# The order of PSUM pools at the entry of attention, and two entries of the up projection, in a transformer block on one core

## The chip, the cores and the metric

The kernel runs on one core of a Trainium2 chip. The metric is the device time of one execution in microseconds (us), and lower is better. Engines are called as the profile calls them: PE is the matrix engine and PEld its weight load, DVE is VectorE, ACT is ScalarE, POOL is GpSimd, and SP is the queue that issues most loads. Each engine works off its own list of instructions in order; where an instruction waits, all behind it on the same engine wait too.

## The reference

One block for 1024 frames of 1024 features, in float32:

```python
h = rms_norm(x, norm1)
proj = h @ w_in                      # q, k, v of two attentions, forget gates, output gates
o_a = forgetting_attention(...)      # 8 heads x 64, causal, decay by sums of log f
o_b = chunk_band_attention(...)      # 8 heads x 64, own chunk of 64 and the 8 before it
merged = g_a * (o_a @ w_branch_a) + g_b * (o_b @ w_branch_b)
x = x + merged @ w_out
h2 = rms_norm(x, norm2)
x = x + square(relu(h2 @ w_up)) @ w_down      # w_up 1024 x 4096, w_down 4096 x 1024
return rms_norm(x, final_norm)
```

## The kernel before

Activations lie transposed, features on the 128 partitions and frames along the free axis in two halves `h` of 512. Every float32 operand is split into a high part (a rounding cast, names ending in `h` or starting with `wh`, `th`) and a low part (value minus high part, names ending in `l` or starting with `wl`, `tl`). A product is then three passes on PE: high x high, high x low, low x high (`product`, L216). The high part of a weight is cast on ACT, its low part is a subtraction on POOL (`split_w`, L163 and L165).

The large products are done in units by one level of Strassen's scheme. A unit (`strassen_steps`) takes four raw quarters of weights (`wr`, loaded from `wall`), makes four sums of them on POOL (`S1`, `S2`, `S3`, `S4`, at L186, L188, L203, L206), splits the seven operands, and runs seven products into four PSUM banks `u0` to `u3`. With activations called `B11, T2, T1, T3, B21, B22, T4`, the products come in the order A11, S2, S1, S3, A12, S4, A22, and DVE and ACT combine the banks between them (L577 to L590). When product 3 (S3) is done, bank 1 is final; products 4, 5 and 6 make banks 0, 2 and 3 final. Raw quarters have four buffers, sums three, and `wh` and `wl` six each, so the seventh weight of a unit, A22, takes the buffer of the first one, A11.

What sets the order of instructions: a scheduler arranges everything that isn't marked, by its own model of time. Instructions through `VO, TO, AO, GO, LO` keep the order in which the code is written. `tc.issue_after(x)` keeps an instruction behind `x`.

Two places matter here.

**The entry of attention.** The last unit of the projections (gate unit 7) works in the four banks of the PSUM pool `psd0`, while the first head's scores run between its products in other banks. Its result in bank `u3` is the last to be ready; DVE scales it (`zt`, L403), and ACT issues its store to `z_dram` (L406). When `psd0` is closed, three pools are opened over its four banks: `pst` (2 banks, transposed probabilities `pt`), `psv` (1 bank, the products `pv` of probabilities and values) and `psg` (1 bank, gate products, and each third `pt` in the first heads). A new tile in a bank waits for the last reader of the bank's old tile. Gate unit 7 has its result `u2` in the first bank, `u3` in the second, `u0` in the third and `u1` in the fourth, since the buffers of `psd0` are dealt out in turn and six single tiles came before the units. For each group of probabilities, PE transposes blocks into `pt` (each T of the order strings), ACT makes `th` (H), DVE makes `tl` (L), and PE multiplies with the values (P).

**The entry of the up projection.** The products with `w_out` are just over; DVE and ACT still make the operands of the first up unit from the last blocks. Unit 28 is the first of 16 units and unit 29 the second. Unit 28 starts on blocks 0 to 2 of its first four products (`START2`) and then takes block 3 of each, whose operands come last (`late_operands`, L1028 to L1037, splits at L278 and L279). After product 3 it does the column sums for the second norm (`norm2_stat`: PE multiplies the squares in `rstd` with `ones`, `n_s`, L266; DVE and ACT turn them into a reciprocal root, L239 to L243, L272, L273); after product 6 the root is spread over partitions (`n_b`) and copied to `rstd` (L1092), and only then do the results of unit 28 leave PSUM (L1101). The weights of unit 29 are held back by `behind=late`, where `lows` is the list of all instructions that made a low part `wl`. Right after unit 28, `lows[-1]` is `wl` of its A22, `lows[-3]` that of its A12.

Of the kernel before, what the change touches and what calls it, by code (L numbers as in the profile page):

```python
# [87 lines left out]
def hs(h):  # L88
    return slice(h * HALF, (h + 1) * HALF)
# [3 lines left out]
def hybrid_block(ctx: ExitStack, tc: tile.TileContext, xT, xN, g1, wall, wf, fb, relb, g2, g3, outT):  # L93
# [17 lines left out]
    def pool(stack, name, side, bufs=1, **kw):  # L111
        return stack.enter_context(tc.tile_pool(name=name, bufs=bufs, side=side, reuse_waits="tile", **kw))

    def psum(stack, name, bufs, side="left"):
        return stack.enter_context(tc.tile_pool(name=name, bufs=bufs, space=PSUM, side=side, reuse_waits="tile"))
# [43 lines left out]
    lows = []  # L159
# [13 lines left out]
    def strassen_w(u, eng, want=ALL):  # L173

        q, sums, out = {}, {}, {}

        def raw(n):
            if n not in q:
                q[n] = quarter(u, n)
            return q[n]  # L180

        def total(name):
            if name not in sums:
                t = sums[name] = wp.tile([P, HALF], F32, tag="ws", name=f"{name}_{u}", bufs=SUMS)
                if name == "S1":
                    eng.tensor_tensor(t, raw(3), raw(2), op=ALU.add)  # L186
                else:
                    eng.tensor_tensor(t, total("S1"), raw(0), op=ALU.subtract)  # L188
            return sums[name]

        if "S2" in want and "A12" in want:
            for n in (0, 1, 3, 2) if want[1] == "A12" else (0, 3, 2, 1):
                raw(n)
        for name in want:
            if name in ("A11", "A12", "A22"):
                src = raw(int(name == "A12") + 2 * int(name == "A22"))
            elif name in ("S1", "S2"):
                if "S2" in want:
                    total("S2")
                src = total(name)  # L200
            elif name == "S3":
                src = raw(3)
                eng.tensor_tensor(src, raw(0), src, op=ALU.subtract)  # L203
            else:
                src = total("S2")
                eng.tensor_tensor(src, raw(1), src, op=ALU.subtract)  # L206
            out[name] = split_w(src, f"{u}_{name}", eng=eng)
        return out

    def product(bank, first, pairs, part=False, eng=T):  # L210

        n = len(pairs) * 3
        t = 0
        for w, x in pairs:
            for wi, xi in ((0, 0), (0, 1), (1, 0)):
                done = eng.matmul(bank, w[wi], x[xi], start=(first and t == 0), stop=(t == n - 1 and not part),  # L216
                                  skip_group_check=part or not first)
                t += 1
        return done.ins
# [41 lines left out]
    def norm_stat(ps_pool, name, acc, eng=T):  # L261

        ps = ps_pool.tile([P, HALF], F32, tag="d", name=f"{name}_s")
        n = acc.shape[1] // P
        for c in range(n):
            eng.matmul(ps[:, c:c + 1], acc[:, c * P:(c + 1) * P], ones, start=True, stop=True)  # L266
        return rms(name, ps, n)

    def rms(name, ps, n=4):

        y, v, t = cpool.tile([P, 2, 4], F32, tag="nr", name=f"{name}_r", bufs=2)[:, 0, 0:n], ps[:, 8:8 + n], ps[:, 16:16 + n]
        V.tensor_scalar(v, ps[:, 0:n], EPS, None, op0=ALU.add)  # L272
        A.activation(y, ps[:, 0:n], AF.Sqrt, bias=epsb)  # L273
        newton(name, v, y, t)
        return y
# [10 lines left out]
    xstack, pstack, astack = ExitStack(), ExitStack(), ExitStack()  # L286
# [249 lines left out]
    def strassen_unit(*args, **kw):  # L536
        for _ in strassen_steps(*args, **kw):
            pass

    def strassen_steps(u, ps_pool, mk, out, start=(), between=None, before=None, cut=0, behind=(), eng=T):  # L540

        def weights(*args):
            with ExitStack() as order:
                for ins in behind:
                    order.enter_context(tc.issue_after(ins))
                return strassen_w(u, *args)

        ws = weights(V if between else G, ALL[:cut] if cut else FIRST if between else ALL)
        late, out_ = [], out
        if before:
            out = lambda *a: late.append(a)
        banks = {}
        for b in (0, 2, 3, 1) if between else range(4):
            banks[b] = ps_pool.tile([P, HALF], F32, tag="d", name=f"u{u}_{b}")
        p1, u2, c22 = mk("p1"), mk("u2"), mk("c22")
        done, steps = None, [(n, range(4)) for n in range(7)]
        if start:  # L560
            more = (0, 4, 1, 2, 3, 5, 6) if between else range(7)
            steps = [(n, range(3)) for n in start] + [(n, (3,) if n in start else range(4)) for n in more]
        for i, (n, ks) in enumerate(steps):
            if i >= cut:
                yield done
            if cut and i == cut:
                ws = weights(G, ALL[cut:])
            wn, xn, b, first = PRODS[n]
            wh, wl = ws[wn]
            done = product(banks[b], first and 0 in ks, [((wh[:, k, :], wl[:, k, :]), xop[xn, k]) for k in ks],  # L570
                           3 not in ks, eng if i >= cut else T)
            if 3 not in ks:
                continue
            if n == 3 and before:
                before[0]()
            if n == 0:
                A.copy(p1, banks[0])  # L577
            elif n == 1:
                V.tensor_tensor(u2, banks[1], p1, op=ALU.add)
            elif n == 2:  # L580
                V.tensor_tensor(c22, banks[2], u2, op=ALU.add)  # L581
            elif n == 3:
                V.tensor_tensor(banks[1], banks[3], c22, op=ALU.add)  # L583
                out(1, 1, banks[1])
            elif n == 4:
                if between:
                    between()
                out(0, 0, banks[0])
            else:
                V.tensor_tensor(banks[b], banks[b], u2, op=ALU.add)  # L590
                out(*((0, 1) if n == 5 else (1, 0)), banks[b])
        if before:
            before[1]()
            for a in late:
                out_(*a)
# [40 lines left out]
    def project_gate(g, **kw):  # L636
        return strassen_steps(U_GATE + g, psd[1 - next(units) % 2], etile,
                              lambda row, h, src: gate_out(src, 2 * g + row, h,
                                                          G if g in GPOOL and (row, h) != (0, 0) else V), **kw)
# [70 lines left out]
    o3 = [[opool.tile([P, HALF], F32R, tag=f"o3{t}{h}", name=f"o3{t}{h}") for t in "hl"] for h in range(2)]  # L710
    apq.append(pool(astack, "apq1", "right"))
    apv, ap0 = [pool(astack, n, "right") for n in ("apv", "ap0")]
    pst = psum(astack, "pst", 2)
    psv = psum(astack, "psv", 1)
    psg = psum(astack, "psg", 1)

    ab_w = {}

# [256 lines left out]
    psm = [psum(ctx, f"psm{n}", 4) for n in range(2)]  # L975
# [39 lines left out]
    accs = [rstd[:, hs(h)] for h in range(2)]  # L1015

    def etile3(name):
        p = ep2[len(ep2[1:]) * (next(turn) % 2)]
        return p.tile([P, HALF], F32, tag="e", name=name, bufs=8)
# [64 lines left out]
    ep2.append(pool(hstack, "ep3", "left"))  # L1084
    n2 = []

    def norm2_stat():
        n2.extend(norm_stat(psm[1], f"n2_{h}", accs[h]) for h in range(2))

    def norm2():  # L1090
        for h in range(2):
# [3 lines left out]
    late = ()  # L1095
    for u in range(16):
        got = {}

        def out(row, h, src):
            v = etile3("v")  # L1100
            V.scalar_tensor_tensor(v, src, 0.0, rstd[:, hs(h)], op0=ALU.max, op1=ALU.mult)  # L1101
            A.activation(v, v, AF.Square)  # L1102
            got[row, h] = v
            if (row, h) != (0, 1):
                store(a_dram[{(0, 0): XI["B11"], (1, 0): XI["B21"], (1, 1): XI["B22"]}[row, h], u], v)
            for n, a, b in {(0, 1): (("T1", (0, 1), (0, 0)), ("T3", (1, 1), (0, 1)), ("T2", (1, 1), "T1")),
                            (1, 0): (("T4", (1, 0), "T2"),)}.get((row, h), ()):
                t = got[n] = etile3("at")
                V.tensor_tensor(t, got[a], got[b], op=ALU.subtract)
                store(a_dram[XI[n], u], t)  # L1110

        strassen_unit(U_UP + u, psm[u % 2], etile3, out, start=() if u else START2, before=None if u else (norm2_stat, norm2),
                      behind=late)

        late = () if u else (lows[-3].ins,)
    hstack.close()
    kstack.close()

# [42 lines left out]
    accs, begun = [rstd[:, hs(h)] for h in range(2)], set()  # L1161
# [185 lines left out]
```

## Time and profile before

| what | time |
|---|---|
| median of three timed runs | 1427.55 us (1426.97 to 1428.85) |
| the profiled execution | 1430.48 us |
| its span, first to last instruction | 1428.5 us |
| granted clock of PE, mean | 0.995 of full speed |
| PE busy | 1400.7 us (98%) |
| DVE, POOL, ACT busy | 885.1, 812.2, 706.6 us |

Times inside the execution are counted from the start of its span. In rows of the timeline the first number is the start, the second the duration, then engine, line, operation, output<-inputs, shape and count; in brackets stands how long the engine was idle before it and what ended that. Matmuls follow each other at shorter distances than their durations, since they overlap in the array. A granted clock (PEclk) of 0.50 means that PE ran at half speed.

### The profile page before, as it was taken

To read this page: it belongs to the slowest core of one execution; us is meant where nothing else is said; L and a number is where in the kernel's file an instruction comes from. 1 tells how busy PE (TensorE), PEld (TensorE's weight loads), DVE (VectorE), ACT (ScalarE), POOL (GpSimd) and SP (SyncE) were. 2 spreads that over 40 slices of the span, in tenths; PEclk is the share of its full clock that TensorE was granted. 3 is DMA by queue.
4 is the path that set the end of the run, shared out by engine and by line. 5 is a ranking of instruction groups with operands and counts; after the bars stand their busy time and mean duration, and the time that the engine had idled before them with its cause. 6 is when DMAs were issued, how large, how long until landed. Compare 5 with 4: busy or idle time off the path is not lost.

```text
span 1428.5 us, 20411 instructions
## 1 busy us (share of the span) xinstructions
PE 1400.7 (98%) x6676; PEld 1168.7 (82%) x6676; DVE 885.1 (62%) x1389; ACT 706.6 (49%) x1361; POOL 812.2 (57%) x639
## 2 busy tenths in 40 slices
PE   9999999999999999999999999999999999999996
PEld 6788888888878888888888888888888888888885
DVE  7756445543258887776655855545555559998644
ACT  8534333343358887775454543333333444444653
POOL 0477777778832233113724677777777545567564
PEclk9999999999999999999999999999999999999998
DMA  8546667773454668886644244444444784678263
GB/s 282 154 116 194 187 196 219 204 198 121 147 169 147 185 209 248 246 257 215 213 162 146 68 166 151 155 154 157 148 154 169 252 269 156 178 234 225 81 221 118
DMA packets 132820, 259.75 MB, mean 182 GB/s; under 512 B 18594, under 2 KB 20642, under 8 KB 129642
## 3 DMA queue, kind: packets, MB, share of 16 engines
q1 hardware_dynamic: 84570, 172.79, 38.6%
q10 hardware_dynamic: 44944, 77.78, 17.2%
q0 software_dynamic: 3200, 7.88, 2.5%
q8 instruction: 52, 0.85, 0.2%
q14 instruction: 54, 0.44, 0.1%
HBM read 172.70 MB, written 85.69 MB: 181 GB/s over the span
## 4 chain that ended last, share of the span: by engine, by line
PE 87%; DVE 3%; issue 3%; ACT 2%; POOL 2%; DMA 2%; SPq 0%; POOLq 0%; ACTq 0%; DVEq 0%
PE u L216 44%; PE dS L216 12%; PE dA L216 5%; PE o L216 5%; PE s L106 5%; PE pv L106 4%; PE pt L106 3%; PE m L106 3%; PE m L216 3%; POOL wl_A L165 1%; PE u L106 1%; DMA xg<-xT 1%; DMA xT<-a_dram 1%; ACT p L106 1%; PE vtp L627 0%
## 5 line engine op out<-in xcount | busy, mean ns | idle before, releaser
L165 POOL TENSOR_TENSOR wl_A<-wr,wh_A 128x512 fp32r<-128x512 f32 x118 | 158.4, 1352 | 94.0 <-ACT wh_A L163 77.0
L165 POOL TENSOR_TENSOR wl_S<-S,wh_S 128x512 fp32r<-128x512 f32 x102 | 136.0, 1337 | 32.9 <-ACT wh_S L163 32.3
L163 ACT CAST wh_S<-S 128x512 fp32r<-128x512 f32 x105 | 64.6, 621 | 114.0 <-PE u L216 53.9
L163 ACT CAST wh_A<-wr 128x512 fp32r<-128x512 f32 x105 | 65.0, 620 | 88.7 <-PE u L216 55.8
L106 DVE TENSOR_TENSOR tl<-pt,th 128x512 fp32r<-128x512 f32 (+1 forms) x144 | 90.5, 641 | 25.9 <-ACT th L106 24.4
L165 POOL TENSOR_TENSOR wl_S<-ks,wh_S 128x512 fp32r<-128x512 f32 x48 | 69.1, 1501 | 53.4 <-ACT wh_S L106 50.0
L590 DVE TENSOR_TENSOR u<-u,u 128x512 f32<-128x512 f32 x70 | 48.8, 698 | 76.0 <-PE u L216 73.6
L106 ACT ACTIVATE p<-s,mn 128x640 f32<-128x640 f32 (+3 forms) x120 | 84.4, 703 | 16.6 <-DVE mn L106 15.5
L106 ACT CAST th<-pt 128x512 fp32r<-128x512 f32 (+1 forms) x144 | 77.6, 551 | 24.5 <-PE pt L106 22.3
L106 PE MATMUL pt<-ident,p 128*128 128x128 f32 x528 | 78.1, 274 | 1.2 <-DVE zt L403 1.1
L186 POOL TENSOR_TENSOR S<-wr,wr 128x512 f32<-128x512 f32 x35 | 46.3, 1324 | 54.8 <-DMA wr<-wall 50.2
L106 PEld LDWEIGHTS pt<-ident,p 128*128 128x128 f32 x528 | 62.2, 141 | 11.0 <-PE pv L106 2.0
L106 PE MATMUL s<-qk 128*128 128x384 f32 (+2 forms) x192 | 58.6, 360 | 8.1 <-ACT p L106 7.3
L165 POOL TENSOR_TENSOR wl_A<-ka,wh_A 128x512 fp32r<-128x512 f32 x32 | 45.1, 1419 | 35.6 <-ACT wh_A L106 34.1
L278 ACT CAST qkh<-qk 128x512 fp32r<-128x512 f32 x32 | 19.9, 621 | 87.5 <-DMA qk_dram<-qkl 34.2
L1102 ACT ACTIVATE v<-v 128x512 f32<-128x512 f32 x64 | 40.4, 632 | 45.1 <-DVE v L1101 42.9
L924 POOL TENSOR_TENSOR on<-on,lo 128x512 f32<-128x512 f32 x7 | 9.0, 1292 | 92.7 <-ACT lo L106 92.7
L106 PE MATMUL pv<-th,v 128*128 128x512 f32 (+3 forms) x180 | 61.3, 348 | 0.1
L583 DVE TENSOR_TENSOR u<-u,c 128x512 f32<-128x512 f32 x35 | 24.5, 699 | 59.4 <-PE u L216 57.3
L106 PE MATMUL pv<-tl,v 128*128 128x512 f32 (+3 forms) x180 | 56.8, 335 | 0.2 <-DVE tl L106 0.2
L1101 DVE SCALAR_TENSOR_TENSOR v<-u,rstd 128x512 f32<-128x512 f32 x64 | 43.9, 688 | 20.1 <-PE u L216 18.1
L581 DVE TENSOR_TENSOR c<-u,u 128x512 f32<-128x512 f32 x35 | 24.2, 691 | 50.7 <-PE u L216 48.9
(445 smaller groups left out, 4742.2 us busy)
## 6 DMA issues: line engine op xcount, KB each, us to landing
wr<-wall SPq DMA_DIRECT2D x233, 256.0 KB
a_dram<-at ACTq DMA_DIRECT2D x64, 256.0 KB
xT<-a_dram SPq DMA_DIRECT2D x64, 256.0 KB
qk<-qk_dram SPq DMA_DIRECT2D x15, 1024.0 KB
qk_dram<-qkh ACTq DMA_DIRECT2D x96, 128.0 KB
a_dram<-v ACTq DMA_DIRECT2D x48, 256.0 KB
xB<-a_dram SPq DMA_DIRECT2D x44, 256.0 KB
z_dram<-zt ACTq DMA_DIRECT2D x32, 256.0 KB
```

Of the source, the lines that this page charges most:

```text
L106: return lambda *a, **kw: tc.keep_in_program_order(getattr(self.eng, name)(*a, **kw))
L163: (act.tensor_copy if act is G or act is V else act.copy)(wh, src)
L165: lows.append(eng.tensor_tensor(wl, src, wh.bitcast(F32), op=ALU.subtract))
L186: eng.tensor_tensor(t, raw(3), raw(2), op=ALU.add)
L216: done = eng.matmul(bank, w[wi], x[xi], start=(first and t == 0), stop=(t == n - 1 and not part), skip_group_check=part or not first)
L278: A.copy(dst[0], src)
L581: V.tensor_tensor(c22, banks[2], u2, op=ALU.add)
L583: V.tensor_tensor(banks[1], banks[3], c22, op=ALU.add)
L590: V.tensor_tensor(banks[b], banks[b], u2, op=ALU.add)
L924: G.tensor_tensor(o, o, lows_o[pr], op=ALU.add)
L1101: V.scalar_tensor_tensor(v, src, 0.0, rstd[:, hs(h)], op0=ALU.max, op1=ALU.mult)
L1102: A.activation(v, v, AF.Square)
```

## The change

The three PSUM pools are opened in the order `psg`, `psv`, `pst`. The sums for the second norm are emitted half by half, the first behind product 3 and the second behind product 4 of unit 28. The weights of unit 29 are held behind the last low part of unit 28, not the third from last.

```diff
-            if n == 3 and before:
-                before[0]()
+            if n in (3, 4) and before:
+                before[0](n - 3)
...
-    pst = psum(astack, "pst", 2)
-    psv = psum(astack, "psv", 1)
-    psg = psum(astack, "psg", 1)
+    psg, psv, pst = [psum(astack, n, b) for n, b in (("psg", 1), ("psv", 1), ("pst", 2))]
...
-    def norm2_stat():
-        n2.extend(norm_stat(psm[1], f"n2_{h}", accs[h]) for h in range(2))
+    def norm2_stat(h):
+        n2.append(norm_stat(psm[1], f"n2_{h}", accs[h]))
...
-        late = () if u else (lows[-3].ins,)
+        late = () if u else (lows[-1].ins,)
```

The number of instructions is the same on every engine, and their order on PE, DVE and SP too. It differs in two places, on POOL and on ACT, both at the entry of the up projection; at the entry of attention one wait differs.

POOL at the entry of the up projection, before (`28` and `29` are the units, the last number of a name is a buffer's own):

```order
L165 TENSOR_TENSOR wl_28_S4_8664<-S2_28_8640,wh_28_S4_8662 128x512
L186 TENSOR_TENSOR S1_29_8845<-wr29_3_8834,wr29_2_8836 128x512
L188 TENSOR_TENSOR S2_29_8844<-S1_29_8845,wr29_0_8832 128x512
L203 TENSOR_TENSOR wr29_3_8834<-wr29_0_8832,wr29_3_8834 128x512
L165 TENSOR_TENSOR wl_28_A22_8668<-wr28_2_8632,wh_28_A22_8666 128x512
L165 TENSOR_TENSOR wl_29_A11_8842<-wr29_0_8832,wh_29_A11_8840 128x512
L165 TENSOR_TENSOR wl_29_S2_8850<-S2_29_8844,wh_29_S2_8848 128x512
```

And the same stretch now:

```order
L165 TENSOR_TENSOR wl_28_S4_8664<-S2_28_8640,wh_28_S4_8662 128x512
L165 TENSOR_TENSOR wl_28_A22_8668<-wr28_2_8632,wh_28_A22_8666 128x512
L186 TENSOR_TENSOR S1_29_8845<-wr29_3_8834,wr29_2_8836 128x512
L165 TENSOR_TENSOR wl_29_A11_8842<-wr29_0_8832,wh_29_A11_8840 128x512
L188 TENSOR_TENSOR S2_29_8844<-S1_29_8845,wr29_0_8832 128x512
L203 TENSOR_TENSOR wr29_3_8834<-wr29_0_8832,wr29_3_8834 128x512
L165 TENSOR_TENSOR wl_29_S2_8850<-S2_29_8844,wh_29_S2_8848 128x512
```

The low part of unit 28's A22 now stands ahead of all three sums of unit 29 (the row at L203 is S3), and that of unit 29's A11 behind the first sum. On ACT the two casts `wh_29_S2` and `wh_29_S1` moved behind the two small roots of the norm (L273); on PE the column sums of both halves stand where they stood.

PE at the entry of attention, before, with the engines that each row waits for (DMAHW2 is a transfer):

```order
L106 MATMUL pt<-ident,p_0_3953 128x128 [waits DVE_49]
L106 MATMUL pt<-ident,p_1_3959 128x128
L106 MATMUL pt<-ident,p_2_3981 128x128
L106 MATMUL pt<-ident,p_3_3987 128x128
L106 MATMUL pt<-ident,p_1_3959 128x128 [waits DVE_49]
L106 MATMUL pt<-ident,p_2_3981 128x128
L106 MATMUL pt<-ident,p_3_3987 128x128 x2
L106 MATMUL pt<-ident,p_2_3981 128x128
L106 MATMUL pt<-ident,p_3_3987 128x128
L106 MATMUL pv<-th,v_4109 128x512 [waits DMAHW2_49,Activation_49]
```

And the last of these rows now:

```order
L106 MATMUL pv<-th,v_4109 128x512 [waits DMAHW2_49,DVE_49,Activation_49]
```

The second group of transposes (its first row is the fifth) had the bank of `u3` before; now it has that of `u1`, and the bank of `u3` goes to `pv`, which therefore waits for DVE as well.

## Prediction

> **What bounds the kernel now.** First the busy times of the page, then the waits of PE over the whole execution, longest first; the rows give engine, tile and line that waited, what ended the wait, us in total, count, longest.
>
> ```profile
> PE 1400.7 (98%) x6676; PEld 1168.7 (82%) x6676; DVE 885.1 (62%) x1389; ACT 706.6 (49%) x1361; POOL 812.2 (57%) x639
> PE s L106 <- ACT p L106: 7.3, 11, 0.9
> ...
> PE pt L106 <- DVE zt L403: 1.1, 1, 1.1
> PE u L216 <- ACT p L577: 0.9, 1, 0.9
> PE u L216 <- DVE T2l L279: 0.8, 1, 0.8
> PE dA L106 <- POOL wl_A L165: 0.7, 1, 0.7
> ```
>
> PE bounds the kernel, and the change can only pay where PE waits or runs slowly. The change touches two of these rows: 1.1 us for a bank of `pt` and 0.8 us for `T2l`. Third I asked for the granted clock in stretches of 3.41 us (start:end, us, then busy us and count of PE, PEld, DVE, ACT, POOL, then PEclk):
>
> ```profile
> 416.93:420.35 3.42, 2.25 (x15) 1.56 (x13) 1.68 (x4) 1.82 (x4) 0.00 (x0) 1.00 0.85 278
> 423.76:427.17 3.41, 2.07 (x12) 1.22 (x10) 1.91 (x7) 2.41 (x7) 0.00 (x0) 1.00 0.35 102
> 427.17:430.58 3.41, 3.16 (x12) 2.97 (x13) 2.37 (x7) 2.52 (x7) 0.00 (x0) 0.50 0.41 154
> 806.05:809.46 3.41, 2.65 (x21) 2.43 (x20) 3.34 (x3) 2.45 (x3) 3.41 (x3) 1.00 0.07 27
> 809.46:812.87 3.41, 3.41 (x10) 2.63 (x9) 3.38 (x5) 0.26 (x1) 3.41 (x4) 0.50 0.36 127
> 812.87:816.28 3.41, 3.41 (x17) 2.78 (x16) 1.84 (x13) 0.95 (x3) 2.54 (x3) 1.00 0.02 5
> ```
>
> Twice PE runs at half speed for 3.41 us, each time right behind 3.41 us in which it did little. The second time is at the up projection's entry: 10 matmuls where 17 start in the next stretch.
>
> **The change, part one: the pools of attention.** The entry of attention in order of time:
>
> ```profile
> 417.71 0.60 PE L106 MATMUL pt<-ident,p 128*128 128x128 f32 x4
> 418.64 0.69 DVE L403 TENSOR_TENSOR zt<-u,rstd 128x512 f32<-128x512 f32 x1
> 419.37 0.33 ACTq L406 DMA_DIRECT2D z_dram<-zt  x1
> 419.39 0.87 PE L106 MATMUL pt<-ident,p 128*128 128x128 f32 x6 [1.08 <-DVE zt L403]
> 419.74 1.35 ACT L106 CAST th<-pt 128x512 fp32r<-128x512 f32 x3 [1.28 <-DVE zt L403]
> 420.38 0.49 PE L106 MATMUL pv<-th,v 128*128 128x512 f32 x1
> 421.10 0.51 PE L106 MATMUL pv<-tl,v 128*128 128x512 f32 x1 [0.23 <-DVE tl L106]
> ```
>
> PE loses 1.08 us because the second `pt` has the bank of `u3`, which DVE reads until 419.33. Now it gets the bank of `u1`, free long before, and the six transposes can follow the first four at 418.15. But the first four were done near 418.3 already, and ACT still cast them only at 419.74: ahead of the cast in ACT's list stands the store of `zt` (L406), which waits for the same `zt` and takes 0.33 us to issue. That order is unchanged. So the first `th` comes at 419.74 as before, the second and third directly behind it (three casts in 1.35 us leave no gap), and `pv` at 420.38. The wait that `pv` gets on DVE ended at 419.33, a microsecond earlier. The 1.08 us that vanish behind the transposes come back ahead of `pv`. Value taken: 0. Bounds: a gain of 1.08 us if ACT were not held by the store, which its own idle row (1.28 us, ended by `zt`) excludes; a loss through the clock, below. When attention is over, the pools of the next stage take the same banks with two waits placed otherwise; PE waits for none of them in the list above, so 0.
>
> **Part two: the sums for the norm, half by half.** On PE the column sums keep their places, on DVE too. Only two casts of unit 29 on ACT come behind the roots. 0.
>
> **Part three: the weights of unit 29.** Here POOL's list changes. What DVE pays for POOL, first at a quiet place, then at the entry:
>
> ```profile
> 787.03 0.68 DVE L279 TENSOR_TENSOR T1l<-xg,T1h 128x512 fp32r<-128x512 f32 x1
> 788.75 1.31 POOL L165 TENSOR_TENSOR wl_S<-S,wh_S 128x512 fp32r<-128x512 f32 x1 [2.19 <-ACT wh_S L163]
> 788.84 1.78 DVE L279 TENSOR_TENSOR B22l<-xg,B22h 128x512 fp32r<-128x512 f32 x1
> ...
> 797.74 1.75 POOL L165 TENSOR_TENSOR wl_S<-S,wh_S 128x512 fp32r<-128x512 f32 x1
> 801.25 1.74 POOL L186 TENSOR_TENSOR S<-wr,wr 128x512 f32<-128x512 f32 x1 [1.76 <-DMA wr<-wall]
> 806.36 3.41 POOL L165 TENSOR_TENSOR wl_A<-wr,wh_A 128x512 fp32r<-128x512 f32 x2
> 801.77 1.78 DVE L279 TENSOR_TENSOR B22l<-xg,B22h 128x512 fp32r<-128x512 f32 x1
> 805.17 1.77 DVE L279 TENSOR_TENSOR T2l<-t,T2h 128x512 fp32r<-128x512 f32 x1
> 801.88 0.62 ACT L278 CAST T2h<-t 128x512 fp32r<-128x512 f32 x1
> 804.33 0.62 ACT L163 CAST wh_A<-wr 128x512 fp32r<-128x512 f32 x1 [1.82 <-PE u L216]
> 805.96 0.28 PE L266 MATMUL n_s<-ones,rstd 128*128 128x1 f32 x2
> 807.00 0.50 PE L216 MATMUL u<-T2l,wh_S 128*128 128x512 f32 x1 [0.77 <-DVE T2l L279]
> 807.57 1.62 PE L266 MATMUL n_s<-ones,rstd 128*128 128x1 f32 x14
> 809.05 0.48 PE L216 MATMUL u<-B21h,wh_A 128*128 128x512 f32 x1
> ```
>
> The same low part on DVE takes 0.68 us while POOL idles (787.03) and 1.78 us while POOL subtracts (788.84). From 801.25 POOL makes the three sums of unit 29, and on DVE `B22l`, `T3l` and `T2l` take about 1.75 us each; `T2l` ends at 806.94, and PE waits 0.77 us for it.
>
> Now the sums stand behind `wl_28_A22`, whose cast runs on ACT at 804.33, because it needs the buffer that PE reads until then. So POOL idles from 799.5 to 804.95. DVE's three low parts run free: `B22l` from 801.77, then `T3l`, then `T2l` (its cast ends at 802.50), each 0.68 us: `T2l` ends at 801.77 + 3 x 0.68 = 803.8. PE wants it behind the first two records of `n_s`, at 805.96 + 2 x 0.11 = 806.18. The wait is gone with 2.4 us to spare, and PE gains 807.00 - 806.18 = 0.82 us. Bounds: 0 (contention at some other place ends at the same time) and 0.82; I take 0.8, as the margin is larger than one contended operation adds (1.1 us).
>
> What comes late instead: POOL starts the sums of unit 29 at 806.25, five microseconds later. The needs stand here:
>
> ```profile
> 809.73 3.14 POOL L165 TENSOR_TENSOR wl_S<-S,wh_S 128x512 fp32r<-128x512 f32 x2
> 814.19 1.28 POOL L165 TENSOR_TENSOR wl_S<-wr,wh_S 128x512 fp32r<-128x512 f32 x1
> 820.64 0.48 PE L216 MATMUL u<-B11h,wh_A 128*128 128x512 f32 x1
> 823.48 0.39 PE L216 MATMUL u<-T2h,wh_S 128*128 128x512 f32 x1
> ```
>
> From 804.95 it has `wl_28_A22`, S1, `wl_29_A11`, S2, S3, `wl_29_S2`: six operations of 1.3 to 1.75 us, so `wl_29_S2` is ready between 812.8 and 815.5 (before: between 811 and 812). PE takes it as the third pass of a product that began at 823.48 and may now begin 2.5 us earlier, at 821. Five microseconds are left. The casts `wh_29_S2` and `wh_29_S1`, behind the roots, need those sums anyway. SP's loads for units 29 and 30 wait for the same POOL operations: the load of `wr29_1` for `wl_28_A22`, now 1.8 us earlier; the first of unit 30 for `wl_29_A11`, about the same. Nothing is lost, 0.
>
> **The clock.** In 806.05 to 809.46 PE ran two 512-column matmuls and sixteen one-column ones, then two more of 512. At full rate these start 0.227 us apart (17 or 18 in 3.41 us), so the four are 0.9 us of work. After that PE ran at half speed for 3.41 us, which costs half of it, 1.70 us. Without the wait, `B21h` starts at 808.24, the same stretch holds 2 + 5 matmuls, 1.6 us. The other stretch that was followed by half speed (423.76) holds 1.17 us counted by columns, and 416.93, which was not, about 1.25 us. So 1.6 us should not trip it: up to 1.70 us more. But the two half-speed stretches begin 382.29 us apart, 112.0 times 3.413: the gate looks at a fixed grid of stretches, and where the grid falls differs between executions. The poor period, 805.96 to 809.05, must nearly fill a cell; sliding the cell, this holds for about 1.1 to 1.5 us of 3.41, an estimate of 4 executions in 10.
>
> [...]
>
> **The sum.** Against the profiled execution (1430.48 us, both half-speed stretches): 0.82 + 1.70 = 2.5 us, to 1428.0. The profile stands 2.93 us above the median 1427.55, nearly two stretches (3.4 us), and the three runs spread over 1.88 us, about one. So the median run probably had none at this place, and there only the 0.8 us count: 1426.75. With the lower level of the two nearer runs (1426.97, 1427.55; mean 1427.26) it is 1426.45. I take 1426.5. From 820 on PE waits almost nowhere (the 0.7 us for `wl_A` in the list is the one wait between units and the tail), so the gain reaches the end.
>
> **Rivals.**
> 1. *The stretch goes in the median too* (0.8 + 1.7): 1425.0. For it: the profiled execution. Against it: the distance of the median from the profile.
> 2. *The clock is not moved by the wait*, because the sixteen one-column sums, which stay, are enough to trip it; the median loses 0.8 us alone, 1426.75. For it: the sums took 1.62 us of the poor cell; against it: 1.6 us of matmuls would now stand beside them. It differs from the forecast by less than the runs spread, and I count it with it. [...]
> 3. *Attention gains its 1.08 us as well*: 1425.4; with rival 1, 1424.0. ACT's store ahead of the cast speaks against it.
> 4. *Slower through the clock at attention*: the transposes move forward, so PE idles 1.6 us in one piece (418.8 to 420.38), and more positions of the grid see a poor cell, by about 0.6 of 3.41 us. A median with one stretch more: 1426.75 + 1.70 = 1428.45. It decides once half of the executions are caught.
> 5. *Slower through POOL*: `wl_29_S2` later than 821.4 holds PE one for one. It needs POOL to lose 6 us more than the worst price above; 3 us of wait would give 1429.7.
> 6. *Nothing changes* (`T2l` late for another cause): 1427.5.
>
> **How the numbers follow.** Forecast with rival 2: 0.58. Rival 1: 0.15, rival 3: 0.07, rival 4: 0.09, rival 5: 0.02, rival 6: 0.09. The range from 1424.8 to 1427.9 leaves out rival 4, 5, and rival 3 with 1. 0.2% is 2.9 us, about what a measurement of this kernel can tell from no change: below 1424.7 lie rival 3 with 1 and part of rival 1, together 0.09; above 1430.4 a little of rivals 4 and 5, 0.03; 0.88 between.
>
> **What would show it.** `B22l`, `T3l`, `T2l` near 802 to 804 with 0.68 us each; POOL idle until about 805; no wait of PE for `T2l`; `B21h` 0.8 us earlier behind block 3 of S3. At attention `th` still right behind ACT's store, with PE's idle time ahead of `pv` rather than ahead of `pt`. The prediction is wrong if ACT casts the first `pt` before the store issues, if PE waits for a `wl` of unit 29, or if the grid of the clock catches other places than I count on.

## The result: 2.5 us less, at the level that was predicted but by a larger gain

| what | kernel before | changed kernel |
|---|---|---|
| median of 20 runs | 1428.89 us (1426.94 to 1431.07) | 1426.36 us (1424.37 to 1429.19) |
| ratio to before, 95% interval | 1 | 0.9983 (0.9976 to 0.9990) |
| the profiled execution | 1430.48 us | 1428.54 us |
| its span | 1428.5 us | 1426.6 us |

The ratio is a gain of 2.4 us (1.4 to 3.4). The forecast, 1426.5 us, is 0.14 us off. But it was reached from 1427.55 us, the median of three runs, by a gain of 1.05 us. Twenty runs put the kernel before 1.34 us higher, and the gain is 1.4 us larger. Two errors of nearly the same size cancel. That the level came out is luck, and the second error is worth finding.

First the busy times and the waits of PE in the changed kernel, as they were shown of before:

```profile
PE 1399.9 (98%) x6676; PEld 1169.3 (82%) x6676; DVE 883.2 (62%) x1389; ACT 707.0 (50%) x1361; POOL 810.5 (57%) x639
...
PE pv L106 <- ACT th L106: 1.4, 1, 1.4
PE u L216 <- ACT wh_S L163: 1.3, 1, 1.3
```

The waits for `T2l` (0.8 us) and for a bank of `pt` (1.1 us) are gone. A wait of `pv` for ACT (1.4 us) has come; the 1.3 us for `wh_S` lie between 38 and 52 us, far ahead of both places.

The entry of the up projection, in groups of DVE, POOL and PE:

```profile
803.82 0.68 DVE L279 TENSOR_TENSOR B22l<-xg,B22h 128x512 fp32r<-128x512 f32 x1
804.42 0.68 DVE L279 TENSOR_TENSOR T3l<-xg,T3h 128x512 fp32r<-128x512 f32 x1
805.03 0.68 DVE L279 TENSOR_TENSOR T2l<-t,T2h 128x512 fp32r<-128x512 f32 x1
805.74 0.69 DVE L1031 TENSOR_TENSOR t<-xg,t 128x512 f32<-128x512 f32 x1
806.47 0.43 DVE L1034 CAST T4h<-t 128x512 fp32r<-128x512 f32 x1
806.93 0.69 DVE L1035 TENSOR_TENSOR T4l<-t,T4h 128x512 fp32r<-128x512 f32 x1
809.68 0.69 DVE L581 TENSOR_TENSOR c<-u,u 128x512 f32<-128x512 f32 x1
...
799.79 1.75 POOL L165 TENSOR_TENSOR wl_S<-S,wh_S 128x512 fp32r<-128x512 f32 x1
807.08 1.70 POOL L165 TENSOR_TENSOR wl_A<-wr,wh_A 128x512 fp32r<-128x512 f32 x1 [5.53 <-PE u L216]
...
808.00 0.28 PE L266 MATMUL n_s<-ones,rstd 128*128 128x1 f32 x2
808.14 0.48 PE L216 MATMUL u<-T2l,wh_S 128*128 128x512 f32 x1
810.17 0.48 PE L216 MATMUL u<-B21h,wh_A 128*128 128x512 f32 x1
812.98 0.39 PE L216 MATMUL u<-B22h,wh_S 128*128 128x512 f32 x1
820.12 0.48 PE L216 MATMUL u<-B11h,wh_A 128*128 128x512 f32 x1
```

Everything here stands 2.04 us later than in the profile of before (the first column sum 808.00, not 805.96), because of the start-up and attention: up to here this execution has three half-speed stretches, at 43, 422 and 429 us, and that of before one, at 427. POOL idles 5.53 us until 807.08, the three low parts take 0.68 us each, and `T2l` is ready 2.4 us before PE takes it at 808.14 without a wait. I measure this place by one stage: from the first column sum to the first product of unit 29 (the last row). It took 820.64 - 805.96 = 14.68 us, and takes 820.12 - 808.00 = 12.12 us: 2.56 us less. That is the gain; from the first product of unit 29 to that of the down projection both kernels take 285.72 us. Near the end the profile of before has one wait more, 0.74 us for `wl_A` at 1407, the 0.7 us in the prediction's list. Below, e9_late_store has this wait with part three and e8_t4_behind lacks it without, so I don't count it to the change.

### The profile page after: what moved, and what is told of

Its sections match the earlier page's. It is cut to its first block, busy times and chain, and to the rows that moved or that the text cites. A ratio compares the mean times of both kernels' runs of the same rounds, so it can differ in the third digit from the quotient of the medians.

```text
span 1426.6 us, 20408 instructions
## 1 busy us (share of the span) xinstructions
PE 1399.9 (98%) x6676; PEld 1169.3 (82%) x6676; DVE 883.2 (62%) x1389; ACT 707.0 (50%) x1361; POOL 810.5 (57%) x639
## 4 chain that ended last, share of the span: by engine, by line
PE 91%; issue 3%; ACT 3%; POOL 2%; DMA 2%; DVE 1%; SPq 0%; POOLq 0%; ACTq 0%; DVEq 0%
PE u L216 44%; PE dS L216 12%; PE dA L216 8%; PE o L216 6%; PE s L106 5%; PE pv L106 4%; PE pt L106 4%; PE m L106 3%; PE m L216 3%; PE u L106 1%; DMA xg<-xT 1%; ACT p L106 1%; POOL wl_A L165 1%; DMA wr<-wall 1%; PE vtp L627 0%
## 5 line engine op out<-in xcount | busy, mean ns | idle before, releaser
L216 PE MATMUL u<-T2h,wh_S 128*128 128x512 f32 x140 | 54.8, 391 | 1.3 <-ACT wh_S L163 1.3
```

## The experiments

All kernels were timed in rounds with the kernel before; ratios are to it. "The stage" is the one just defined, taken from the profiled execution of each kernel.

### The parts one at a time

Part three alone (e1_late):

```diff
-        late = () if u else (lows[-3].ins,)
+        late = () if u else (lows[-1].ins,)
```

> Part three alone: only the weights of unit 29 are held behind the low part of A22; the pools and the sums for the norm stay as before. Theory A (the whole gain is the wait for T2l and the half-speed stretch behind it): the full gain of the change, 2.5 us (ratio 0.9983, between 0.9975 and 0.9990); no wait of PE for T2l, T2l 0.68 us, about 2.5 us before PE wants it. Rival B (the pools carry a share of 1 us): at most 1.5 us (0.9990 to 0.9995). Rival C (the median moved only through the half-speed stretches of other places, by luck of the grid): 0.8 us (0.9994).

Measured: 1426.67 us, ratio 0.9983 (0.9974 to 0.9992), stage 12.12 us, as theory A said. The stage is that of the changed kernel to the hundredth, so part three is the whole gain there. In the traces, PE, DVE, ACT and POOL work off the same instructions in the same order in this kernel and in the changed one: with part three in, the other two parts move nothing. The two casts on ACT that the prediction put down to part two come with part three. Part two alone wasn't run.

Part one alone (e2_pools):

```diff
-    pst = psum(astack, "pst", 2)
-    psv = psum(astack, "psv", 1)
-    psg = psum(astack, "psg", 1)
+    psg, psv, pst = [psum(astack, n, b) for n, b in (("psg", 1), ("psv", 1), ("pst", 2))]
```

> Part one alone: only the order of the three pools is changed. Theory A: 0 within 0.7 us (ratio 0.9995 to 1.0005); ten transposes in one piece, then PE idle about 1.4 us until the first th, which comes about 0.04 us behind the issue of the store of zt as before. Rival B: 1.08 us faster (0.9992). Rival D (the idle piece trips the clock more often): up to 1 us slower (1.0007).

Measured: 1430.63 us, ratio 1.0010 (1.0001 to 1.0019). At the entry of attention 2.66 us from the first transpose to `pv`, as before (2.67): part one gains nothing there, as theory A said. The time, 1.4 us (0.1 to 2.7) above before, is outside A's range and nearest to rival D's (see rival 4 below).

This run gave the clue to the size. Its up projection is that of the kernel before, but its profiled execution had no half-speed stretch there (granted clock 1.00 from 804 to 822). By the prediction the stage should then be 14.68 - 1.70 = 13.0 us. It took 14.43. PE's waits at this place, and the rows of DVE and PE:

```profile
PE u L216 <- DVE c L581: 1.1, 1, 1.1
PE u L216 <- DVE T2l L279: 0.8, 1, 0.8
...
806.92 1.65 DVE L1031 TENSOR_TENSOR t<-xg,t 128x512 f32<-128x512 f32 x1
808.61 1.39 DVE L1034 CAST T4h<-t 128x512 fp32r<-128x512 f32 x1
810.03 1.66 DVE L1035 TENSOR_TENSOR T4l<-t,T4h 128x512 fp32r<-128x512 f32 x1
811.62 0.68 DVE L579 TENSOR_TENSOR u<-u,p 128x512 f32<-128x512 f32 x1
812.33 0.69 DVE L581 TENSOR_TENSOR c<-u,u 128x512 f32<-128x512 f32 x1
...
811.60 0.39 PE L216 MATMUL u<-B21h,wl_A 128*128 128x512 f32 x1
813.07 0.50 PE L216 MATMUL u<-B22h,wh_S 128*128 128x512 f32 x1 [1.09 <-DVE c L581]
```

There is a second wait. POOL's sums of unit 29 slow `T2l` (1.77 us, against 0.68 in the changed kernel), and the low parts that POOL makes behind them slow the three T4 operations (4.70 us, against 1.81 us in the changed kernel). Behind those on DVE stand `u` and `c`, and `c` reads the bank that product S4 (`B22h`) writes next. So PE waits 1.09 us for `c`. In the profile of before this wait was covered:

```profile
812.37 0.69 DVE L581 TENSOR_TENSOR c<-u,u 128x512 f32<-128x512 f32 x1
813.47 0.40 PE L216 MATMUL u<-B22h,wh_S 128*128 128x512 f32 x1
```

The half-speed stretch over the `B21h` products, which start 0.43 us apart in it and 0.23 us apart at full clock, held PE back until 813.47, and `c` was done at 813.06. Two of the kernels below repeat this: e11_pools_store, without a stretch there, has both waits (0.77 and 1.11 us) and a stage of 14.47 us; e5_store_pool_before, with one, waits for `T2l` alone and takes 14.61 us.

### The second wait taken away, and brought back

First the kernel before with only the T4 operations moved (e8_t4_behind). They are held behind the combination of banks that follows `c`:

```diff
-                V.tensor_tensor(banks[1], banks[3], c22, op=ALU.add)
+                final = V.tensor_tensor(banks[1], banks[3], c22, op=ALU.add)
                 out(1, 1, banks[1])
+                if before:
+                    with tc.issue_after(final.ins):
+                        last_t4[0]()
...
+        def t4():
+            V.tensor_tensor(t2, b21, t2, op=ALU.subtract)
...
+        last_t4.append(t4) if k == 3 else t4()
```

> The kernel before, with one edit: DVE makes the three T4 operations of the last block behind the combinations of units' banks (u, c, u) instead of ahead of them. POOL's order, the pools and all else as before. Theory A (behind the wait for T2l stands a second wait, for c, because the three T4 operations, slowed by POOL, hold up c on DVE; it shows only when no half-speed stretch lies over it): T2l still waits 0.75 us; PE waits nowhere for c; from the first column sum to unit 29 13.3 us without a half-speed stretch at that place (14.43 in the pools-alone kernel) and 14.7 with one. Median 0.5 to 0.7 us below the kernel before (1.1 us in those executions that have no stretch, somewhat over half). Theory B (my prediction's count: only T2l and the stretch): no change, 0.0 us, and 14.4 without a stretch.

```profile
PE u L216 <- DVE T2l L279: 0.7, 1, 0.7
...
807.00 0.69 DVE L581 TENSOR_TENSOR c<-u,u 128x512 f32<-128x512 f32 x1
808.93 0.68 DVE L1041 TENSOR_TENSOR t<-xg,t 128x512 f32<-128x512 f32 x1
809.68 1.37 DVE L1043 CAST T4h<-t 128x512 fp32r<-128x512 f32 x1
811.11 1.64 DVE L1044 TENSOR_TENSOR T4l<-t,T4h 128x512 fp32r<-128x512 f32 x1
```

PE still waits 0.7 us for `T2l` and nowhere for `c`; the stage takes 13.06 us without a half-speed stretch, against 14.43. That is theory A's row (13.3). In time, 1428.20 us, ratio 0.9994 (0.9985 to 1.0003): the centre, 0.9 us, agrees with A, but the interval doesn't exclude no change.

Now the other way: the changed kernel with contention put back. POOL repeats the subtraction for `wl` of unit 28's S4, twice (e6_pool2) and four times (e6_pool4), which changes no engine's order:

```diff
-        lows.append(eng.tensor_tensor(wl, src, wh.bitcast(F32), op=ALU.subtract))
+        for _ in range(1 + (2 if name == f"{U_UP}_S4" else 0)):
+            done = eng.tensor_tensor(wl, src, wh.bitcast(F32), op=ALU.subtract)
+        lows.append(done)
```

> The changed kernel, in which POOL repeats the subtraction for wl of unit 28's S4 four more times in the place where it idles (801.5 to 807), so that it works beside DVE as it did before, without any sum of unit 29 being moved. Theory A (what the change gains at the up projection comes from POOL's idle time beside DVE's low parts and T4 operations): B22l, T3l, T2l take 1.78 us each again, T2l ends at 809.05 and PE waits 0.9 us for it; the T4 operations end near 813.8, c near 815.1, and PE waits 1.2 us more for c: 14.2 us from the first column sum to unit 29 (12.12 in the changed kernel), median 2.1 us above the changed kernel, as slow as before, 1428.5. Theory B (only the wait for T2l counts): 13.1 us and 1.0 us above it, 1427.4. Theory C (the gain comes from the order of the sums or their loads, not from POOL's idle time): 12.1 us, 1426.4.

> The changed kernel, in which POOL repeats the subtraction for wl of unit 28's S4 twice more, right behind itself (by the run with four repeats this runs on without a gap, so here from about 799.8 to 805.0 in the times of the changed kernel). It tells how much contention the margin of 2.4 us ahead of T2l takes. Theory A (DVE's delay costs PE nothing until the margin is used up): two operations of DVE take 1.77 us instead of 0.68, B22l, T3l and T2l move by 2.2 us and still come in time by 0.2 us; c moves too, and stays ahead of PE's need at 813: no wait of PE for T2l, T3l or c, 12.1 to 12.4 us from the first column sum to unit 29, median as the changed kernel, 1426.4 (to 1427). Theory B (each operation of POOL beside DVE costs PE its 1.1 us): 14.3 us and 1428.6.

With four, the repeats ran from 797.93 without a gap, earlier than I had counted on. Seven of DVE's operations in a row, from `T1l` at 798.44 to `T2l`, took 1.75 to 1.78 us each; in the changed kernel only `T1l` does. PE waited for three operands:

```profile
797.93 8.52 POOL L166 TENSOR_TENSOR wl_S<-S,wh_S 128x512 fp32r<-128x512 f32 x5
806.02 0.50 PE L218 MATMUL u<-T2h,wh_S 128*128 128x512 f32 x1 [0.64 <-ACT T2h L280]
808.73 0.50 PE L218 MATMUL u<-T3l,wh_S 128*128 128x512 f32 x1 [1.97 <-DVE T3l L281]
810.41 0.79 PE L218 MATMUL u<-T2l,wh_S 128*128 128x512 f32 x1 [0.84 <-DVE T2l L281]
811.43 2.98 PE L268 MATMUL n_s<-ones,rstd 128*128 128x1 f32 x14
...
806.32:809.73 3.41, 1.29 (x6) 0.67 (x4) 3.41 (x3) 2.45 (x4) 3.30 (x3) 1.00 0.11 38
809.73:813.14 3.41, 2.73 (x11) 2.54 (x12) 3.34 (x3) 0.00 (x0) 3.41 (x4) 0.50 0.11 39
813.14:816.56 3.42, 3.42 (x12) 2.94 (x13) 3.38 (x8) 0.26 (x1) 1.44 (x2) 0.50 0.19 60
816.56:819.97 3.41, 3.41 (x10) 2.64 (x9) 1.55 (x11) 1.85 (x4) 2.48 (x2) 0.50 0.05 17
```

The last four rows are stretches of 3.41 us (PE, PEld, DVE, ACT, POOL busy, then the granted clock). The stretch from 806.32 holds six matmuls, and three stretches at half speed follow one another, though PE is busy throughout two of them. The time is 1436.54 us, ratio 1.0052 (1.0039 to 1.0065); from the start of unit 28 to unit 29 it is 31.22 us, against 22.55 in the changed kernel. All three theories missed the size; that POOL beside DVE is the mechanism, and not the order of the sums, is supported, since POOL's order was not changed.

With two, the dose is finer, and it splits the two waits:

```profile
797.67 5.14 POOL L166 TENSOR_TENSOR wl_S<-S,wh_S 128x512 fp32r<-128x512 f32 x3
805.22 1.69 POOL L166 TENSOR_TENSOR wl_A<-wr,wh_A 128x512 fp32r<-128x512 f32 x1 [2.40 <-PE u L218]
805.09 0.68 DVE L281 TENSOR_TENSOR T2l<-t,T2h 128x512 fp32r<-128x512 f32 x1
805.80 1.66 DVE L1033 TENSOR_TENSOR t<-xg,t 128x512 f32<-128x512 f32 x1
805.89 0.28 PE L268 MATMUL n_s<-ones,rstd 128*128 128x1 f32 x2
811.96 0.50 PE L218 MATMUL u<-B22h,wh_S 128*128 128x512 f32 x1 [0.91 <-DVE c L583]
```

`T2l` is ready at 805.77, just in time, and PE doesn't wait for it, as A said. But the delay brings the T4 operations beside POOL's next operations, and PE waits 0.91 us for `c`, which A had denied. In the changed kernel `c` has a margin no smaller than that of `T2l` (ready at 810.37, wanted at 812.98); what A left out is that the T4 operations, once beside POOL, add 2.9 us of their own (4.70 instead of 1.81 us). The stage takes 13.34 us, between A's 12.1 to 12.4 and B's 14.3. The kernel takes 1427.05 us, ratio 0.9990 (0.9981 to 0.9999): by the ratios 1.0 of the 2.4 us is lost, though the two intervals overlap. So each of the two waits was seen without the other: e8 has `T2l` alone (13.06), this one `c` alone (13.34), e2 both (14.43), the changed kernel none (12.12, as in the three other kernels with part three alone or with a moved store). The two single waits are worth 0.94 and 1.22 us, together 2.16 of the 2.31 us between e2 and the changed kernel.

### The clock taken away

The kernel before with five matmuls that nobody reads, so that the poor cell is fuller (e7_fill5):

```diff
+                idle = psm[1].tile([P, HALF], F32, tag="d", name="idle")
+                for _ in range(5):
+                    T.matmul(idle, wh[:, 0, :], xop["T3", 0][0], start=True, stop=True)
```

> The kernel before with five more matmuls of 512 columns whose result nobody reads (idle), one ahead of the last T2l products and four ahead of the other fourteen column sums, so that PE has more to do in the period that trips the clock. One of them lies in the wait for T2l, the other four are 0.9 us on PE's path. Theory A (a second wait for c of 1.1 us follows, set by DVE, not by PE): no half-speed stretch; the four cost nothing, since PE then waits 0.2 us for c instead of 1.1: 14.5 us from the first column sum to unit 29; median 0.1 us below the kernel before (0.25 us in those executions that had the stretch). Theory B (my prediction's count: the median execution has no stretch and loses only the wait for T2l): 0.9 us above the kernel before; in an execution with the stretch 0.8 us below it (13.9 us).

Here all sixteen column sums came behind the fillers, so the stage is counted from the start of unit 28: 24.88 us to unit 29, where the kernel before takes 25.13 in its profile (with the stretch), e2 24.88 (without) and the changed kernel 22.55. There is no half-speed stretch at this place (granted clock 1.00) and no wait for `c` among PE's waits; product S4 starts 0.12 us late at most, right behind `c`:

```profile
812.57 0.69 DVE L584 TENSOR_TENSOR c<-u,u 128x512 f32<-128x512 f32 x1
813.31 0.50 PE L216 MATMUL u<-B22h,wh_S 128*128 128x512 f32 x1
```

So an execution without the stretch is 0.25 us shorter here, and four matmuls on PE's path cost nothing: what holds product S4 there is DVE's `c`. That is A. In time, 1429.82 us, ratio 1.0004 (0.9995 to 1.0013), which doesn't tell A from B.

### The entry of attention

The prediction said that ACT's store of `zt`, ahead of the cast, swallows what the pool order gains. Four kernels issue that one store from POOL's queue, with each combination of parts one and three:

```diff
-        store(z_dram[c, :, hs(h)], t)
+        (load_r if (c, h) == (15, 0) else store)(z_dram[c, :, hs(h)], t)
```

> The kernel before with only the last store of zt moved to POOL's queue; the pools in the old order. Theory A: the first th comes early, but the second group of transposes still waits for the bank of u3 until zt is read, and pv stands behind it in PE's list: pv at most 0.3 us earlier, 0 to 0.3 us faster (0.9998 to 1.0000). If the store alone were the whole hold, 1.0 us (0.9993).

> The changed kernel, and the last store of zt (the one ahead of the first th in ACT's list) is issued from POOL's queue, which is idle there. Theory A (ACT's wait for zt in front of the store hides the pool order): the first th comes right behind the last read of the exponentials, about 1.2 us earlier; tl then waits for DVE's zt, so pv starts about 1.0 us earlier; 1.0 us faster than the changed kernel, 3.5 us than before (0.9975), and fewer half-speed stretches at attention. Rival (PE or the exponentials bound the entry, not the store): pv moves by less than 0.3 us, the time that of the changed kernel (0.9983).

> Part three alone (weights of unit 29 behind the last low part of unit 28, pools in the old order) with the last store of zt issued from POOL's queue instead of ACT's. Theory A (the store holds ACT's cast by 0.36 us at the entry of attention, and with the old pool order nothing more; the shorter poor period is met by fewer positions of the clock's grid, 0.1 of them where part three alone has 0.5): 2.3 us from the first transpose to pv (2.67 in part three alone), median 0.36 to 1.1 us below part three alone, 1425.6 to 1426.3, and above the changed kernel with the same store (1424.65) by 0.6 us or more. Theory B (the store pays only where pv and not pt waits for zt): 2.7 us at the entry and 1426.7.

> Part one alone (the pool order of attention) with the last store of zt issued from POOL's queue instead of ACT's, to complete the pairs with and without the pool order. Theory A (behind the store lies the wait that the pool order removes, so that the order pays once the store is away, 0.58 us, and costs time through the clock only while the store is there): 1.73 us from the first transpose to pv (2.31 with the old order and the same store), no half-speed stretch at that place in most executions; median 0.6 to 0.9 us below the old order with the same store (ratio to before 0.9997), that is 0.9991 to 0.9993 of the kernel before. Theory B (the pool order costs time at some other place, as it seemed to in the run of it alone, 1.4 us): 1.001 of the kernel before.

| kernel | pool order | part three | store on | first transpose to `pv` | median | ratio to before (95%) |
|---|---|---|---|---|---|---|
| before | old | no | ACT | 2.67 us | 1428.89 us | 1 |
| e2_pools | new | no | ACT | 2.66 us | 1430.63 us | 1.0010 (1.0001 to 1.0019) |
| e5_store_pool_before | old | no | POOL | 2.31 us | 1428.49 us | 0.9997 (0.9988 to 1.0006) |
| e11_pools_store | new | no | POOL | 1.73 us | 1427.89 us | 0.9992 (0.9984 to 1.0001) |
| e1_late | old | yes | ACT | 2.67 us | 1426.67 us | 0.9983 (0.9974 to 0.9992) |
| changed kernel | new | yes | ACT | 2.67 us | 1426.36 us | 0.9983 (0.9976 to 0.9990) |
| e9_late_store | old | yes | POOL | 2.31 us | 1425.55 us | 0.9975 (0.9966 to 0.9984) |
| e4_store_pool_after | new | yes | POOL | 1.73 us | 1424.65 us | 0.9973 (0.9964 to 0.9981) |

First the entry in the changed kernel, then in e4_store_pool_after:

```profile
418.18 1.26 PE L106 MATMUL pt<-ident,p 128*128 128x128 f32 x10
419.12 0.69 DVE L403 TENSOR_TENSOR zt<-u,rstd 128x512 f32<-128x512 f32 x1
419.84 0.33 ACTq L406 DMA_DIRECT2D z_dram<-zt  x1
420.21 1.35 ACT L106 CAST th<-pt 128x512 fp32r<-128x512 f32 x3 [1.28 <-DVE zt L403]
420.85 0.50 PE L106 MATMUL pv<-th,v 128*128 128x512 f32 x1 [1.41 <-ACT th L106]
```

```profile
418.02 1.25 PE L106 MATMUL pt<-ident,p 128*128 128x128 f32 x10
418.67 1.34 ACT L106 CAST th<-pt 128x512 fp32r<-128x512 f32 x3
418.95 0.69 DVE L403 TENSOR_TENSOR zt<-u,rstd 128x512 f32<-128x512 f32 x1
419.74 0.47 PE L106 MATMUL pv<-th,v 128*128 128x512 f32 x1 [0.47 <-ACT th L106]
419.94 0.60 POOL L406 DMA_DIRECT2D z_dram<-zt  x1 [13.75 <-ACT th L106]
```

With the store on ACT the ten transposes run in one piece, and ACT casts the first only behind the store: the wait moved from `pt` to `pv`. With the store away ACT casts 0.65 us behind the first transpose and no longer behind `zt`. In the rows the order alone is worth 0, the store alone 0.36 us, both 0.94 us: the gain of the order lay behind the store, as theory A of these runs said. In time the differences between neighbouring rows of the table are about as large as their intervals, so the times alone don't show it. A had put e9_late_store at least 0.6 us above e4_store_pool_after, partly through the clock; by the ratios it is 0.3 us, which shows nothing of the clock's share. e4_store_pool_after, the changed kernel with the store on POOL, is the fastest of all: 4.34 us below the median of before in its batch (1428.99 us), by its ratio 3.9 us (2.7 to 5.1).

## Why the prediction came out, and which step was mis-sized

- **`T2l`, contention and POOL's idle time.** As predicted, row by row, if 2.04 us are added: POOL back at 807.08 (predicted 804.95 + 2.04 = 806.99), `T2l` ready at 805.71 (805.84), `B21h` at 810.17 (810.28). The 0.8 us are there.
- **The clock, the step that failed.** "So the median run probably had none at this place, and there only the 0.8 us count." The step priced an execution without the half-speed stretch by the first wait alone. The runs showed a second wait in its place, for `c`, which e2_pools has with 1.09 us. Its term was missing. It could have been read off the profile of before, in the rows shown above: `c` starts at 812.37 and takes 0.69 us, so it ends at 813.06; and the twelve `B21h` products, from 809.05 at 0.227 us each, would end at 811.8 with a full clock. By this estimate the stretch hid a wait of 1.2 us. With it the gain of the stage is 2.31 us in an execution of before without the stretch and 2.56 us in one with it, nearly the same, and the ratio's 2.4 us lie between. What looked like rival 1, the stretch going in the median too, is reached by either way.
- **The grid of the clock.** Seen in both profiles. The half-speed stretches of before begin at 427.17, 809.46 and 1420.45 us, 382.29 and 610.99 us apart, those of the changed kernel at 43.49, 422.36 and 429.19, 378.88 and 6.83 us apart: 112.0, 179.0, 111.0 and 2.0 times 3.413 us. From 422.36 to 809.46 it is 113.4 times, so the grid does fall differently in the two. How little work in a stretch brings on the half speed was my estimate from three stretches (0.9 and 1.17 us of matmuls ahead of half speed, 1.25 not); no run measures it.
- **The base.** The distance of the profiled execution from the median of three runs, 2.93 us, was read as nearly two stretches. (A third one in that profile, from 1420.45, lies behind PE's last matmul and costs PE nothing.) Twenty runs put the profiled execution 1.59 us above the median, about one stretch, and the argument from that distance falls. With the higher base the prediction would have counted the stretch in more executions, but the wait for `c` would still have been missing. The base was 1.34 us too low and the gain 1.4 us too small: that these cancel is luck.
- **Casting behind the store.** Right: 0 at the entry (2.67 us in both), with the idle time ahead of `pv`, as the last section of the prediction asked for.
- **Rival 4, slower through the clock at attention.** The sign is seen once: e2_pools is 1.4 us slower (0.1 to 2.7). In the pair with part three the order shows no such loss (e1_late 0.9983, changed kernel 0.9983, each to within 1.3 us), and e11_pools_store, with the new order and the store away, shows none either (0.9992). The profiles of e1_late (old order) and e2_pools (new order) both have a half-speed stretch at 421, the changed kernel has two at attention (422.36 and 429.19), before one (427.17). Of the timed executions only the mean clock is on record, not the places, so the price of the order stays open.
- **POOL's later sums.** Right: PE waits for no `wl` of unit 29; the list of waits of the changed kernel has none.

## What to carry to other kernels

When a stall or a slow stretch is to go, list every operand that is needed while it lasts, and compare each one's time of arrival with the time at which the engine would want it at full speed; the next-latest is the bound, and the list of waits doesn't show it. If a neighbour's work slows an engine, count all operations of that engine under it that its work slows, not only the one that is waited for. If a wait moves from one row to another of the same size, look at what stands ahead of the new releaser in its own queue: here a store of 0.33 us on ACT that waited for an unrelated tile.

## What the runs showed of the hardware that I had not expected

- Stretches at half speed can follow one another: with four repeats there were three in a row (809.73 to 819.97), the last two over a PE that was busy all the time. Why the third came behind a stretch in which PE was never idle wasn't tried.
- POOL works through repeats back to back: five in e6_pool4 took 8.52 us, 1.70 us each beside DVE; two subtractions of the changed kernel, from 813.71, took 1.28 us each, with DVE idle until 815.90. In the kernel before, `T1l`, `B22l`, `T3l`, `T2l` (798.25 to 806.94) and the two subtractions for T4 (806.98, 810.09) each began while POOL was in an operation that had begun earlier, and took 1.64 to 1.79 us; in the changed kernel the last five of these began with POOL idle and took 0.68 to 0.69 us. The cast `T4h` took 1.38 us before and 0.43 us in the changed kernel. Where DVE began first, POOL took longer: in the changed kernel `T4l` at 806.93 takes 0.69 us, and POOL's subtraction at 807.08 takes 1.70 us. `u` and `c`, which read a PSUM bank, take 0.68 and 0.69 us with POOL busy throughout (811.62 and 812.33 in e2_pools): not every operation of DVE is slowed.
- The one-column sums take longer at half speed too: the fourteen `n_s` took 1.62 us in the kernel before and 2.98 us in e6_pool4.
